# A two-layer decoder step: attention operands split into two halves at the accumulator, keys turned by DMA, scores paced by the page transposes, and another mixing ratio for the last recurrence

## The chip, the cores and the metric

One core of one Trainium2 chip. The metric is the device time of one execution in microseconds (us), the median of several executions. Engines: PE (TensorE matmul; PEld is its weight load), DVE (VectorE), ACT (ScalarE), POOL (GpSimd), SP (SyncE, which issues nearly all DMAs).

## What is computed

One inference step of a two-layer decoder, over a prompt of 2048 tokens and 8 decoding sequences of 4 new tokens each (32 tokens, "the sample"). The parts that matter here, from the reference:

```
qa, fa, ia, ga, qb, kb, vb, gb, fb = _split(h @ w_in, ...)        # layer 0, one input projection
o_a, s_a = gated_linear_chunked(...)                               # HGRN2 recurrence, 4 heads
o_b = fox_attend(qb, kb, vb, log_sigmoid(fb + b_fox))              # 4 heads of 128
out = concatenate([o_a * silu(ga), o_b * silu(gb)]) @ w_out        # layer-0 output projection
...
# fox_prompt: logits = q k^T * scale + c_t - c_s, causal softmax, times v
# fox_sample: the same of 4 new tokens against 16 pages of 128 cached keys per sequence, page_table picks the pages
o, s = gated_linear_chunked(...); return o @ w_out                 # layer 1: GLA, 4 heads of 128 x 256
return rmsnorm(x, final_norm), kb_h, vb_h, ...                     # the keys and values are outputs too
```

All data is f32. Every large product is made of three f16 passes: an operand x is split into hi = f16(x) and lo = f16(x - hi), and `mm3` (L595 to L597) adds hi*hi, hi*lo and lo*hi in f32.

## The kernel before, in words

The program runs through four stages. **Even** (0 to 852 us of the trace): the input projection of layer 0 for the first and then the second half of the tokens, mixed with the HGRN2 recurrences of the four heads (`lin(0)` to `lin(3)`). A projection is a list of units with names: "Bq", "Bk", "Bv" and "Bg" are the attention's query, key, value and gate columns, two units each (a pair of heads). Each unit's PSUM tiles are `pf_Bq...` (features on partitions) or `pt_Bk...`, `pt_Bv...` (tokens on partitions). **Fox** (852 to 1292): the attention. **Layer-0 output projection and layer 1** (1292 to 2150), and **the last output projection with the final norm** (2150 to 2361).

What the even stage does with the attention's operands (`mk_bq`, `mk_bkv`, from L980): a query tile is evicted by ACT as f32 with its scale (L991) and stored feature-major to DRAM (`qTd`). A key or value tile is evicted by DVE (L1020) as f32, stored to its output (L1034) and, for values, to `vd` as well (L1037). Keys are then turned: four PE transposes per pair of token tiles into a PSUM tile `BkT` (L1045), an ACT eviction with scale (L1049), and a store to `kTd` (L1051).

In fox two generators share the engines. `fox_prompt` walks 16 groups (4 heads x 4 blocks G of 512 query tokens). A group's q, k and v are loaded as f32 (`raw_q`, `raw_k`, `raw_v`, L1321) after the first of four score rows of the group ahead, and split on chip at rows 2 and 3: ACT scales v (L1330), ACT makes hi (L1331), POOL makes lo (L1332), each 128x512. An `issue_after` on the last exponential and the last key copy of the sample holds these splits back in the queues. Then come: scores `s` on PE (L1378 on, through `mm3`), bias and row maximum on DVE (L1385), the exponential on ACT (L1393), the scale by one over the sum on POOL (L1401) of a tile `L`, its transposes `pt` on PE (L1421), their split on ACT (`th`, L1428) and DVE (`tl`, L1429), and the product with v into `fo`. `L` tiles live in a pool "P" of 17 buffers. `fox_sample` loads 128 pages of keys and then of values (`pgcache_fox_k`, `pgcache_fox_v`, 256 KB each, L1515), turns the keys by PE (four transposes of one page row make a "turn": `pkt`, L1545), copies them (`kts`, ACT and DVE by turns, L1548 and L1549), multiplies them with the queries (`sc`, L1603) and the probabilities with the values (`pv`, L1684). `until` (L1316) interleaves the two generators by their estimated costs and the ratio FOX_P to FOX_S.

What sets the order: the Python order in which instructions are given to the framework, and a scheduler of the framework that orders each engine's queue by priorities and by its own estimate of readiness; `issue_after(x)` is a hint that an instruction is put behind x in that order, not a wait. Within a queue an engine runs strictly in order, so an instruction that waits holds everything behind it.

Last stage: `mux` (L75) interleaves the last head's recurrence of the second half, `lins[1](3)`, with `third()` (the output projection of the first half, tiles `pt_o`) by LIN3_B to 88000 (L2127). The recurrence's results leave as `py_C133`, `y_C`, are stored to `yT`, come back as `yr`, and are turned into the operand `act` (L1784, L1785) of the last tiles `pt_o`.

## Time and profile before

| | |
|---|---|
| runs of the kernel before | 2357.75, 2358.47, 2360.31 us, median 2358.47 |
| the profiled execution | 2362.66 us, its span in the trace 2361.0 us, mean granted clock 0.988 |
| busy shares over the span | PE 96%, PEld 68%, DVE 59%, ACT 46%, POOL 35%; DMA queue 1 47% |
| instructions | 58204 |

How to read the views. A row of a table of windows gives a stretch's start and end, its length, the busy time (and instruction count) of PE, PEld, DVE, ACT and POOL, the mean granted PE clock as a share of full speed, the mean busy share of the 16 DMA engines (parts in parallel can take it a little over 1), and the GB/s moved. A row of groups gives line, engine, operation, tiles out<-in, shapes and count, then busy us and mean ns of one, then the engine's idle time just before them with what ended it. In a timeline the two first numbers are start and duration in us; idle time before the row stands in brackets. PE matmuls are pipelined: a row's duration contains a latency, so the cost of one in a series is the distance of starts.

### The profile page before, as it was taken

The numbers are of one execution on the slowest core, as the hardware profiler recorded it, in microseconds if no ns is written. First come the engines' busy times: TensorE is split into PE (matmuls) and PEld (weight loads), VectorE is DVE, ScalarE is ACT, GpSimd is POOL, SyncE is SP. The second block draws the span as 40 slices with busy tenths as digits, with TensorE's granted clock in tenths as the row PEclk, the third lists the DMA queues.
The fourth block names the chain that finished last, engine by engine and source line by source line (L and its number), as shares of the span: only waits on it lengthen the run. The fifth ranks groups of instructions, "written<-read, shape, count | busy, mean of one in ns | idle before, by whom it ended". The sixth has DMA issues, their size and how long they took to land. (4 is left out here: it accounts for less than half of the span.)

```text
span 2361.0 us, 58204 instructions
## 1 busy us (share of the span) xinstructions
PE 2267.8 (96%) x23124; PEld 1614.2 (68%) x23124; DVE 1404.2 (59%) x3225; ACT 1090.5 (46%) x2372; POOL 816.5 (35%) x858
## 2 busy tenths in 40 slices
PE   7999999999999999999999999999899999999998
PEld 6677667855655876655446888667677666667877
DVE  7756567536764548566767444366775655557554
ACT  6434354233333127566677443546544544544333
POOL 2333333102212225234557244144552432232222
PEclk9999999999999999999999999999999999999999
DMA  6232235855431276776874778523234431115453
GB/s 199 65 95 74 83 105 157 199 144 157 141 118 60 85 218 214 256 248 204 268 236 141 255 215 244 141 82 117 74 113 109 107 97 57 51 53 167 152 194 148
DMA packets 358003, 344.89 MB, mean 146 GB/s; under 512 B 90993, under 2 KB 300722, under 8 KB 357730
## 3 DMA queue, kind: packets, MB, share of 16 engines
q1 hardware_dynamic: 356226, 336.64, 47.0%
q8 instruction: 182, 2.98, 0.5%
q0 software_dynamic: 1504, 4.52, 0.5%
q14 instruction: 91, 0.75, 0.1%
HBM read 248.73 MB, written 79.63 MB: 139 GB/s over the span
## 5 line engine op out<-in xcount | busy, mean ns | idle before, releaser
L597 PE MATMUL pt_o<-w_o,act 128*128 128x256 f16 x1024 | 281.1, 274 | 4.0 <-DVE act L1785 3.6
L596 PE MATMUL pt_o<-w_o,act 128*128 128x256 f16 x1024 | 281.1, 275 | 1.5 <-POOL w_o L356 1.5
L595 PE MATMUL pt_o<-w_o,act 128*128 128x256 f16 x1024 | 281.2, 275 | 0.9 <-ACT sg1C L652 0.9
L595 PEld LDWEIGHTS <-act 128*128 128x128 f16 x2304 | 227.3, 99 | 39.5 <-DMA act<-xs 5.4
L597 PEld LDWEIGHTS <-act 128*128 128x128 f16 x2304 | 227.4, 99 | 38.0 <-DVE act L1785 5.0
L596 PEld LDWEIGHTS <-act 128*128 128x128 f16 x2304 | 227.4, 99 | 31.5 <-issue 1.5
L595 PE MATMUL pt_Cv<-w_Cv,act 128*128 128x256 f16 (+1 forms) x512 | 142.2, 278 | 3.7 <-DMA act<-xs 3.6
L762 POOL TENSOR_TENSOR kA<-kA,fA 128x512 f32<-128x512 f32 (+1 forms) x56 | 79.0, 1411 | 186.8 <-PE gl_A L728 139.9
L596 PE MATMUL pt_Cv<-w_Cv,act 128*128 128x256 f16 (+1 forms) x512 | 142.1, 278 | 0.0
L597 PE MATMUL pt_Cv<-w_Cv,act 128*128 128x256 f16 (+1 forms) x512 | 142.0, 277 | 0.0
L762 POOL TENSOR_TENSOR kC<-kC,fC 128x512 f32<-128x512 f32 (+1 forms) x56 | 83.7, 1495 | 154.8 <-PE gl_C L728 106.1
L1393 ACT ACTIVATE L<-L,nm,kc 128x512 f32<-128x512 f32 (+3 forms) x160 | 118.2, 741 | 34.7 <-DVE nm L1391 31.4
L1401 POOL TENSOR_SCALAR L<-L,nm 128x512 f32<-128x512 f32 (+3 forms) x160 | 99.1, 634 | 63.5 <-DVE nm L1397 22.9
L1428 ACT ACTIVATE th<-pt 128x512 f16<-128x512 f32 (+3 forms) x159 | 80.5, 528 | 63.0 <-PE pt L1421 62.2
L1429 DVE TENSOR_TENSOR tl<-pt,th 128x512 f16<-128x512 f32 (+3 forms) x159 | 94.5, 608 | 21.9 <-ACT th L1428 20.9
L1421 PE MATMUL pt<-ident,L 128*128 128x128 f32 x544 | 91.3, 279 | 6.8 <-POOL L L1401 4.1
L1421 PEld LDWEIGHTS pt<-ident,L 128*128 128x128 f32 x544 | 66.8, 143 | 32.9 <-DVE tl L1429 8.3
L1545 PEld LDWEIGHTS pkt<-ident,pgcache_fox_k 128*128 128x128 f32 x512 | 58.3, 142 | 41.7 <-issue 25.1
L1879 ACT ACTIVATE vC<-pt_Cv,kc 128x512 f32<-128x512 f32 (+1 forms) x40 | 23.9, 599 | 133.8 <-PE pt_Cv L597 133.8
L1545 PE MATMUL pkt<-ident,pgcache_fox_k 128*128 128x128 f32 x512 | 75.7, 281 | 6.0 <-DVE kts L1549 3.9
L595 PE MATMUL pt_Av<-w_Ai,act 128*128 128x256 f16 x256 | 71.1, 278 | 0.5 <-ACT act L590 0.5
L596 PE MATMUL pt_Av<-w_Ai,act 128*128 128x256 f16 x256 | 70.9, 277 | 0.4 <-DVE w_Ai L349 0.4
(957 smaller groups left out, 6751.4 us busy)
## 6 DMA issues: line engine op xcount, KB each, us to landing
pgcache_fox_k<-in_cache_fox_k SPq DMA_DIRECT2D x128, 256.0 KB, 4.3
pgcache_fox_v<-in_cache_fox_v SPq DMA_DIRECT2D x128, 256.0 KB, 4.0
yr<-yT SPq DMA_DIRECT2D x16, 1024.0 KB, 7.1
x1d<-xo SPq DMA_DIRECT2D x48, 256.0 KB, 3.9
wr_Aqf<-in_w_in_even SPq DMA_DIRECT2D x64, 128.0 KB, 3.2
wr_o<-in_w_out_even SPq DMA_DIRECT2D x32, 256.0 KB, 6.1
xo<-in_x_prompt SPq DMA_DIRECT2D x32, 256.0 KB, 3.6
wr_Cv<-in_w_in_odd SPq DMA_DIRECT2D x32, 256.0 KB, 3.9
```

The source lines that it names most:

```text
L595: nc.tensor.matmul(ps, lh[0], rh[0], start=first, stop=False)
L596: nc.tensor.matmul(ps, lh[0], rh[1], start=False, stop=False)
L597: return nc.tensor.matmul(ps, lh[1], rh[0], start=False, stop=last)
L762: nc.gpsimd.tensor_tensor(kv[:, :, 0], kv[:, :, 0], t1.to_broadcast([P, nb, w]), ALU.mult)
L1393: self.last_exp = nc.scalar.activation(lt[:, :w], lt[:, :w], AF.Exp, bias=nm[:, 0:1], scale=ib, accum_out=nm[:, 2 + j : 3 + j])
L1401: nc.gpsimd.tensor_scalar(lt[:, :w], lt[:, :w], nm[:, 1:2], 2.0**14, ALU.mult, ALU.mult)
L1421: nc.tensor.transpose(pt[:, w : w + P], rows[b][s // 4][0][:, (s % 4) * P : (s % 4 + 1) * P], self.ident)
L1428: nc.scalar.activation(th[:, a:w], pt[:, a:w], AF.Copy),
L1429: nc.vector.tensor_tensor(tl[:, a:w], pt[:, a:w], th[:, a:w], ALU.subtract)))
L1545: nc.tensor.transpose(pk[:, j * P : (j + 1) * P], pgs[j][:, h * P : (h + 1) * P], self.ident)
L1879: r = nc.scalar.activation(v[h][:, g : g + cnt], ps[:, :, :256], AF.Copy, scale=c)
```

## The change

- **Even stage.** A query tile is split where it leaves PSUM: ACT writes hi as f16, DVE writes lo as f16 (one `scalar_tensor_tensor`), one DMA stores both to `qd`. A key or value tile keeps its f32 eviction and output store, and gets two ACT and two DVE instructions per pair of token tiles (each 128x256) that write hi and lo; they go token-major to `kd` and `vd`. The PE transposes and the ACT eviction of the prompt's keys are gone; those of the 32 sample tokens stay. A new column `cu` holds the product of the two scales. The sample's q, k and v are kept in f32 (`qs`, `ks`, `vs`).
- **Fox loads.** q and v are loaded as f16 pairs by plain DMAs, k by `dma_start_transpose` of a 512 x 256 f16 block per group, all without a split on chip. Pool "P" has 20 buffers, q 3, k 6, v 6.
- **Order in fox.** A score tile is put behind the page transposition that lies PKLAG = 16 turns back (`self.pks`). The hints on the splits are gone with them.
- **Last stage.** LIN3_B goes from 21000 to 27000: more steps of the recurrence per step of the output projection.

The core of the diff:

```diff
+PKLAG = 16
-LIN3_B = 21000.0
+LIN3_B = 27000.0
...
-                            nc.scalar.activation(t[:, :m], ps, AF.Copy, scale=self.fsc["q", hp][0])
-                            store_cols(self.qTd[h], t, c0, m)
+                            up, few = self.fsc["q", hp][0], max(0, c0 + m - HALF)
+                            u = t.bitcast(F16).rearrange("p (x t) -> p x t", x=2)[:, :, : m - few]
+                            nc.scalar.activation(u[:, 0], ps[:, : m - few], AF.Copy, scale=up)
+                            nc.vector.scalar_tensor_tensor(u[:, 1], ps[:, : m - few], up, u[:, 0], ALU.mult,
+                                                           ALU.subtract)
...
                     nc.vector.tensor_scalar(t[:m, g % 2 : g % 2 + cnt], ps[:, :, :256], c, None, ALU.mult)
+                    if m == P:
+                        u = held[1]
+                        for j in range(cnt):
+                            src = ps[:, j, :256].rearrange("p (h d) -> p h d", h=2)
+                            hi, lo = (u[:, g % 2 + j, :, x] for x in range(2))
+                            nc.scalar.activation(hi, src, AF.Copy, scale=self.cu[which, hp])
+                            nc.vector.scalar_tensor_tensor(lo, src, self.cu[which, hp], hi, ALU.mult, ALU.subtract)
...
-                    if which == "k":
+                    if which == "k" and m < P:
                         pk = pps.tile([P, 2, 256], F32, tag="gr", name=f"BkT{hf}{hp}{g}")
...
-            fx = Pool(f0, {"vh": 5, "vl": 5, "P": 17, "th": 4, "tl": 4, "sg": 3, "y": 1},
-                      Pool(f1, {"raw": 6, "caus": 1, "qh": 2, "ql": 2, "kh": 5, "kl": 5, "cb": 2, "st1": 12, "cm": 2}))
+            fx = Pool(f0, {"v2": 6, "P": 20, "th": 4, "tl": 4, "sg": 3, "y": 1},
+                      Pool(f1, {"caus": 1, "q2": 3, "k2": 6, "cb": 2, "st1": 12, "cm": 2}))
...
-        if scale is not None:
-            nc.scalar.activation(r, r, AF.Copy, scale=scale)
-        nc.scalar.activation(hi, r, AF.Copy)
-        nc.gpsimd.tensor_tensor(lo, r, hi, ALU.subtract)
...
+            nc.sync.dma_start(q, self.qd[h][:, :, gs])
+            nc.sync.dma_start_transpose(k, self.kd[gs, h].rearrange("t x d -> t (x d)"))
             bias(h, G)
...
-                self.last_pe = self.mm3(ps[:, :w], q, [x[:, :w] for x in K[h, j]], True, True)
+                with ExitStack() as st:
+                    if len(self.pks) > PKLAG:
+                        st.enter_context(self.tc.issue_after(self.pks[-1 - PKLAG].ins))
+                    self.last_pe = self.mm3(ps[:, :w], q, [x[:, :w] for x in K[h, j]], True, True)
...
-                nc.tensor.transpose(pk[:, j * P : (j + 1) * P], pgs[j][:, h * P : (h + 1) * P], self.ident)
+                last = nc.tensor.transpose(pk[:, j * P : (j + 1) * P], pgs[j][:, h * P : (h + 1) * P], self.ident)
+            self.pks.append(last)
```

Three places in the order. The first is SP's queue at the start of fox, where the loads of the first groups stand ahead of the first page (`raw_...` and `k2_...` are loads for head and block, `out_fox_v_p` the outputs of the last value tiles, `cb` a bias row). Before:

```order
L1321 DMA raw_q00_10833<-qTd_71 128x512
L1321 DMA raw_k00_10835<-kTd_72 128x512
L1347 DMA cb0_10837<-cbd_75 128x512
L1321 DMA raw_v00_10839<-vd_74 128x4x128
L1321 DMA raw_q01_10870<-qTd_71 128x512
L1321 DMA raw_k01_10872<-kTd_72 128x512
L1034 DMA out_fox_v_p<-Bv112_10693 128x2x256
L1037 DMA vd_74<-Bv112_10693 128x2x256
```

And of the change:

```order
L1352 DMA q2_00_10916<-qd_71 128x2x512
L1353 DMA_TRANSPOSE k2_00_10917<-kd_72 128x2x512
L1057 DMA out_fox_v_p<-Bv110_10702 128x2x256
L1345 DMA cb0_10921<-cbd_78 128x512
L1352 DMA q2_01_10940<-qd_71 128x2x512
L1353 DMA_TRANSPOSE k2_01_10941<-kd_72 128x2x512
L1059 DMA vd_73<-Bvs110_10703 128x2x512
L1345 DMA cb0_10921<-cbd_78 128x512
L1352 DMA q2_02_11018<-qd_71 128x2x512
L1353 DMA_TRANSPOSE k2_02_11019<-kd_72 128x2x512
L1057 DMA out_fox_v_p<-Bv112_10761 128x2x256
```

Key loads became transposing DMAs; three more of them (`k2_03`, `k2_10`, `k2_11`) follow, so that six stand in SP's queue ahead of the first page load, while the value loads moved behind pages.

The second is PE's queue in the middle of fox, where the page turns `pkt203` and `pkt210` come; `sc` are the sample's products, `fo` and `pt` the prompt's. Before, the page turns follow one another with only the sample's work between:

```order
L1634 MATMUL sc1_12413<-suf_11679,sel_11608 32x128 x7
L1545 MATMUL pkt203_13180<-ident_58,pgcache_fox_k08_13127 128x128
L1545 MATMUL pkt203_13180<-ident_58,pgcache_fox_k09_13129 128x128
L1545 MATMUL pkt203_13180<-ident_58,pgcache_fox_k010_13131 128x128
L1545 MATMUL pkt203_13180<-ident_58,pgcache_fox_k011_13133 128x128
L1545 MATMUL pkt210_13265<-ident_58,pgcache_fox_k18_13257 128x128
L1545 MATMUL pkt210_13265<-ident_58,pgcache_fox_k19_13259 128x128
L1545 MATMUL pkt210_13265<-ident_58,pgcache_fox_k110_13261 128x128
L1545 MATMUL pkt210_13265<-ident_58,pgcache_fox_k111_13263 128x128
L1603 MATMUL sc2_13332<-kts200_13140,qz_11093 32x512
```

With the change the prompt's work stands between the same two turns:

```order
L1534 MATMUL pkt203_13198<-ident_58,pgcache_fox_k011_13151 128x128
L601 LDWEIGHTS v2_03_11270
L601 MATMUL fo03_13036<-th03015_13835,v2_03_11270 128x128
L1418 MATMUL pt1000_13968<-ident_58,L100_13044 128x128
L1418 MATMUL pt1000_13968<-ident_58,L110_13297 128x128
L1418 MATMUL pt1000_13968<-ident_58,L120_13522 128x128
L1418 MATMUL pt1001_13977<-ident_58,L110_13297 128x128
L1418 MATMUL pt1001_13977<-ident_58,L120_13522 128x128
L1534 MATMUL pkt210_13283<-ident_58,pgcache_fox_k18_13275 128x128
```

The prompt's score tiles no longer run ahead of the pages, so that their transposes and products are left for this place. Of the 127 gaps between neighbouring page turns, 54 hold no work of the prompt in the order before (the longest run is 16 turns, from `pkt200` on), and 41 with the change (the longest run 6).

The third is PE's queue in the last stage, where the last head's results `py_C133` leave the recurrence among the tiles of the first half's output projection (`pt_o1000` to `pt_o1036`, 16 tiles of 48 matmuls). Before:

```order
L597 MATMUL pt_o1036_31600<-w_o103_30842,act_18943 128x256
L700 MATMUL py_C1330_31588<-ident_58,on_C133_31567 128x128 x2
L595 LDWEIGHTS act_18943
L595 MATMUL pt_o1036_31600<-w_o103_30842,act_18943 128x256
L596 LDWEIGHTS act_18943
L596 MATMUL pt_o1036_31600<-w_o103_30842,act_18943 128x256
L700 MATMUL py_C1331_31594<-ident_58,on_C133_31567 128x128 x2
```

And with the change:

```order
L601 MATMUL pt_o1030_31299<-w_o103_30765,act_18818 128x256
L704 MATMUL py_C1330_31253<-ident_58,on_C133_31232 128x128 x2
L599 LDWEIGHTS act_18818
L599 MATMUL pt_o1030_31299<-w_o103_30765,act_18818 128x256
L600 LDWEIGHTS act_18818
L600 MATMUL pt_o1030_31299<-w_o103_30765,act_18818 128x256
L601 LDWEIGHTS act_18818
L601 MATMUL pt_o1030_31299<-w_o103_30765,act_18818 128x256
```

The last `py_C1331` moved from behind the 29th matmul of `pt_o1036` to behind the 20th of `pt_o1030`: 28 + 48 + 48 + 29 = 153 matmuls of the projection that stood ahead of it now stand behind it.

More of the change, by code (lines that the diff above doesn't have):

```diff
@@ L1350, in loads @@
             gs = slice(G * 512, (G + 1) * 512)
[L1351 to L1352 removed]
+            q, k, v = (fx.tile([P, 1024], F16, tag=x + "2", name=f"{x}2_{h}{G}") for x in "qkv")
+            q, k = (x.rearrange("p (x t) -> p x t", x=2) for x in (q, k))
+            v = v.rearrange("p (c x d) -> p c x d", c=4, x=2)
+            nc.sync.dma_start(q, self.qd[h][:, :, gs])
+            nc.sync.dma_start_transpose(k, self.kd[gs, h].rearrange("t x d -> t (x d)"))
             bias(h, G)
[L1354 removed]
+            nc.sync.dma_start(v.rearrange("p c x d -> p c (x d)"),
+                              self.vd[gs, h].rearrange("(c s) x d -> s c (x d)", s=P))
+            Q[h, G], K[h, G], V[h, G] = ([x[:, 0], x[:, 1]] for x in (q, k, v.rearrange("p c x d -> p x c d")))
             SG[h, G] = fx.tile([P, 512], F32, tag="sg", name=f"fsg{h}{G}")
             nc.sync.dma_start(SG[h, G], self.sgd[h][:, gs])
[L1358 to L1365 removed]
         def scores(h, G, b):
@@ L1449, in fox_prompt @@
         loads(0, 0)
-        for x in "qkv":
-            split(x, 0, 0)
         pv, ns = iter(()), 0
@@ L1456, in fox_prompt @@
                 rows.append((yield from scores(h, G, b)))
-                if j + 1 < len(groups):
-                    if b == 0:
-                        loads(*groups[j + 1])
-                    elif b == 2:
-                        split("q", *groups[j + 1])
-                        split("k", *groups[j + 1])
-                    elif b == 3:
-                        split("v", *groups[j + 1])
+                if j + 1 < len(groups) and b == 0:
+                    loads(*groups[j + 1])
                 for _ in range(ns // 4):
@@ L1525, in fox_sample @@
         vn = one([TS, 512], "vn")
-        for t, d in ((qs, self.qTd), (kn, self.kTd), (sgs, self.sgd)):
-            nc.sync.dma_start(t, d[:, :, T : T + TS].rearrange("h p t -> p h t"))
-        nc.sync.dma_start(vn, self.vd[T : T + TS])
+        for t, d in ((qs, self.qs), (kn, self.ks), (sgs, self.sgd[:, :, T : T + TS])):
+            nc.sync.dma_start(t, d.rearrange("h p t -> p h t"))
+        nc.sync.dma_start(vn, self.vs)
         with self.tc.issue_after(self.last_l.ins):
@@ L1616, in fox_sample @@
                         new.append(turn(c, b, h, pgs))
-                    if h == 2:
-                        self.last_kt = new[-1][1]
                     yield SC_C
@@ L1721, in fox_scale @@
         nc.vector.reciprocal(up, down)
+        self.cu[which, hp] = self.kcol()
+        nc.vector.tensor_scalar(self.cu[which, hp], c, up, None, ALU.mult)
         if which == "v":
```

67 lines of the change are left out of this document (26 added, 41 removed).

## The prediction

> **What bounds the kernel now.** First the page's list of busy times.
>
> ```profile
> span 2361.0 us, 58204 instructions
> PE 2267.8 (96%) x23124; PEld 1614.2 (68%) x23124; DVE 1404.2 (59%) x3225; ACT 1090.5 (46%) x2372; POOL 816.5 (35%) x858
> ```
>
> PE is busy for 96% of the span; the next engine, DVE, for 59%. So there are two ways to gain: take instructions off PE, or take away some of the few per cent in which it stands still or runs slowly. An average hides where these are, so the second view is the table of windows, cut at the stages.
>
> ```profile
> 0.00:852.00 852.00, 826.55 (x9065) 583.64 (x9066) 506.37 (x1167) 313.04 (x702) 227.57 (x219) 0.99 0.42 119
> 852.00:1292.00 440.00, 411.64 (x2914) 245.18 (x2913) 303.21 (x940) 278.09 (x625) 215.98 (x326) 0.98 0.71 229
> 2150.00:2361.00 211.00, 195.51 (x2162) 169.56 (x2160) 118.51 (x231) 78.74 (x196) 59.94 (x67) 0.97 0.51 169
> ```
>
> PE is idle for 25.5 us of the even stage, 28.4 us of fox and 15.5 us of the last stage. The clock column adds to that: at 0.98 over 440 us fox loses another 8.8 us, so that about 37 us is all that shorter waits could give there. Fox is also where the DMA engines are busiest (0.71). The sum below is made against the profiled execution, 2362.66 us. It is 4.2 us above the median of the runs, 2358.47, and I take those 4.2 us off at the end.
>
> **Even stage: transposes out, evictions in.** These groups (0 to 866 us, shapes apart; fox in the two last) carry the prices.
>
> ```profile
> L1045 PE MATMUL BkT<-ident,Bk 128*128 128x128 f32 x64 | 9.9, 276 | 1.1 <-DVE lf L1015 0.6 <-ACT kts_A L845 0.5
> L1049 ACT ACTIVATE BkS<-BkT,kc 128x512 f32<-128x512 f32 x16 | 11.0, 685 | 56.1 <-PE BkT L1045 53.3 <-issue 2.3 <-ACT scT L736 0.5
> L1020 DVE TENSOR_SCALAR Bv<-pt_Bv,kc 128x256 f32<-128x256 f32 x16 | 7.4, 474 | 0.0
> L991 ACT ACTIVATE Bq<-pf_Bq,kc 128x512 f32<-128x512 f32 x8 | 5.5, 688 | 7.3 <-PE pf_Bq L597 7.3
> L1429 DVE TENSOR_TENSOR tl<-pt,th 128x512 f16<-128x512 f32 x112 | 75.5, 686 | 20.6 <-ACT th L1428 19.9
> L1428 ACT ACTIVATE th<-pt 128x512 f16<-128x512 f32 x112 | 64.0, 590 | 46.6 <-PE pt L1421 46.2
> ```
>
> The 64 prompt transposes leave PE. The 276 ns of one contain a latency; what one costs in a series is the distance of starts, which the page transposes show, the same operation on the same shape:
>
> ```profile
> 1002.37 1.07 PE L1603 MATMUL sc<-kts,qz 128*32 128x512 f32 x8 [0.45 <-DVE kts L1549]
> 1003.37 1.09 PE L1545 MATMUL pkt<-ident,pgcache_fox_k 128*128 128x128 f32 x8
> 1004.81 1.09 PE L1545 MATMUL pkt<-ident,pgcache_fox_k 128*128 128x128 f32 x8 [0.35 <-DVE kts L1549]
> 1006.25 1.06 PE L1603 MATMUL sc<-kts,qz 128*32 128x512 f32 x8 [0.35 <-DVE kts L1549]
> ```
>
> Eight take 1.09 us with one latency of about 0.27 at the end, so 0.82 over seven steps, 0.117 each; 64 of them are 7.5 us, of which I take 7, and the 1.1 us that PE waited ahead of them goes too: **-8**.
>
> Added are 64 hi on ACT and 64 lo on DVE (128x256), and 20 lo on DVE for the queries. No row before shows these; the nearest are L1429's lo (686 ns for 128x512) and L1020's 474 ns for 128x256, so a lo of 128x256 is about 0.45 us and 64 are 29 us, and 20 query tiles at about 0.6 are 12 us: 41 us more on DVE. ACT gets 64 x about 0.38 (half of 590, and a fixed part) = 24 us and loses the 11.0 us of L1049. What hides them is PE's own work in the same place:
>
> ```profile
> 360.00:400.00 40.00, 38.04 (x560) 31.95 (x558) 26.02 (x65) 13.82 (x29) 13.24 (x11) 1.00 0.45 135
> 400.00:475.00 75.00, 75.00 (x732) 66.25 (x731) 42.21 (x84) 25.46 (x56) 15.70 (x13) 1.00 0.79 201
> ...
> 360.00:400.00 40.00, 3.31 (x5) 1.00 0.45 135
> ```
>
> The last row is line L1020 alone. From 400 to 475 PE is never idle and DVE has 33 us left; there the lo's are covered. From 360 to 400, where the recurrence's short steps go back and forth between PE and DVE, DVE is busy for 26 of 40 us and an added lo can stand ahead of a step that PE waits for. Five evictions by L1020 stand there and about as many at the matching place of the second half: some ten pairs of lo at 0.9 us, 9 us at most if each is waited for in full; few will be, since three PSUM buffers of the projection stand between. I take **+2**, with 0 and +6 as ends (a gain is excluded: work is only added). Together **-6**.
>
> **Fox, the start.** The timeline and the window of the first microseconds:
>
> ```profile
> 871.00:879.00 8.00, 5.81 (x20) 2.64 (x21) 3.31 (x14) 5.32 (x13) 6.31 (x9) 0.57 1.02 310
> ...
> 867.50 0.22 PE L595 MATMUL s<-h_k,h_q 128*128 128x128 f16 x1 [0.99 <-DVE Bv L1020]
> 872.54 3.06 SPq L1515 DMA_DIRECT2D pgcache_fox_k<-in_cache_fox_k  x6
> 875.33 0.61 PE L597 MATMUL s<-h_k,l_q 128*128 128x512 f16 x1 [0.43 <-POOL l_q L1332]
> 1487.23 2.10 SPq L565 DMA_TRANSPOSE act<-xs  x1
> ```
>
> POOL is busy for 6.3 of 8 us (it splits, and PE waits for its l_q), and the clock is 0.57: 0.43 x 8 = 3.4 us of PE's speed lost. Without splits on chip I take those **-3**. Against that stand the transposing loads. One costs SP about 2.1 us for 128 x 2048 (`act<-xs`), so about 1.2 for a k block of half that size, against 0.4 for a plain load: six ahead of the first page load are +5 us in a queue that had gaps. Their packets are slower too:
>
> ```profile
> 1475.00:1490.00 15.00, 13.84 (x116) 10.87 (x115) 5.12 (x21) 5.75 (x11) 2.31 (x2) 1.00 1.08 201
> 1001.00:1013.00 12.00, 9.81 (x76) 5.88 (x76) 4.77 (x8) 3.68 (x7) 0.00 (x0) 1.00 0.88 307
> ```
>
> Where transposes and plain loads of layer 1 mix, a full share (1.08) moves 201 GB/s; with pages alone 0.88 moves 307. Per unit of DMA time that is 186 against 349. So a transposed k block of 256 KB takes about twice the 0.75 us of a plain one, 16 blocks some 12 us of DMA time more in a stage that has 0.29 x 440 = 128 us free. Only at the start, with the engines full, is it late: **+2** for pages and first keys (ends 0 and +13, worked out with the slower rival). [...] The start comes to **-1**.
>
> **Fox, the sample alone.** In the rows from 1002 to 1006 above, page turns and scores of the sample have PE for themselves: one step of four turns takes 3.88 us (1002.37 to 1006.25), in which PE starts 8 score and 16 page matmuls, 1.0 + 2 x 0.94 = 2.8 us of its own work. So each step loses 1.1 us, 0.28 a turn, waiting for kts, the copy. In the order 54 of 127 gaps between turns held no prompt work before, and 41 after: 13 x 0.28 = 3.6, **-4** (ends 0 and -10, if the short runs that remain cost less than the long one).
>
> **Fox, ACT and POOL.** What PE waits for, by groups (852 to 1292 us):
>
> ```profile
> L1421 PE MATMUL pt<-ident,L 128*128 128x128 f32 x544 | 91.3, 279 | 6.8 <-POOL L L1401 4.1 <-DVE tl L1429 2.6
> L1545 PE MATMUL pkt<-ident,pgcache_fox_k 128*128 128x128 f32 x512 | 75.7, 281 | 6.0 <-DVE kts L1549 3.9 <-DVE nm L1396 0.8 <-ACT kts L1548 0.7
> L595 PE MATMUL fo<-th,h_v 128*128 128x512 f16 (+3 forms) x174 | 59.0, 339 | 4.6 <-ACT th L1428 3.3 <-DVE mx L1385 0.9 <-DVE fy L1444 0.3
> L596 PE MATMUL s<-l_k,h_q 128*128 128x512 f16 (+3 forms) x160 | 56.0, 351 | 1.2 <-POOL l_k L1332 1.2
> L597 PE MATMUL s<-h_k,l_q 128*128 128x512 f16 (+3 forms) x160 | 55.3, 354 | 0.4 <-POOL l_q L1332 0.4
> ...
> L1330 ACT ACTIVATE raw_v<-raw_v,kc 128x512 f32<-128x512 f32 x16 | 11.4, 712 | 4.4 <-DMA raw_v<-vd 4.4
> L1331 ACT ACTIVATE h_q<-raw_q 128x512 f16<-128x512 f32 x16 | 9.9, 619 | 8.0 <-DMA raw_q<-qTd 8.0
> L1332 POOL TENSOR_TENSOR l_k<-raw_k,h_k 128x512 f16<-128x512 f32 x16 | 18.6, 1160 | 0.0
> ```
>
> The splits are 16 x (0.712 + 3 x 0.62) = 41 us of ACT's 278 and 16 x 3 x 1.16 = 56 us of POOL's 216, each a block of one to three microseconds in an in-order queue that `th` and `L` also pass. PE's waits for those two engines' results are 4.1 + 3.3 + 1.2 + 0.4 = 9.0 us. I take all of them, **-9**: what later delays put in their place is balanced by waits that stand as "DVE tl" but come from ACT's `th` just before. The ends are 0 (PE is late for DVE next, which keeps its 303 us) and -25 (the 37 us of idle time and lost clock, less the 3 at the start and the 8.5 that these rows put down to DVE: 2.6, 0.9, 0.3, 3.9 and 0.8).
>
> **Last stage.** The output projection stops twice, on the operand of the last recurrence's results.
>
> ```profile
> 2271.05 0.27 PE L596 MATMUL pt_o<-w_o,act 128*128 128x256 f16 x1
> ...
> 2272.04 0.27 PE L596 MATMUL pt_o<-w_o,act 128*128 128x256 f16 x1
> 2274.98 0.40 PE L597 MATMUL pt_o<-w_o,act 128*128 128x256 f16 x1 [2.67 <-DVE act L1785]
> ...
> 2277.38 0.39 PE L597 MATMUL pt_o<-w_o,act 128*128 128x256 f16 x1 [0.94 <-DVE act L1785]
> 2270.00:2282.00 12.00, 8.28 (x50) 5.46 (x48) 7.79 (x12) 5.84 (x12) 2.80 (x3) 0.72 0.71 233
> ```
>
> The stops are 2.67 + 0.94 = 3.6 us, and the clock after them, 0.72 over 12 us, costs 3.4 more. A projection matmul takes 0.11 us (nine starts from 2271.05 to 2272.04), so with 153 of them put behind `py_C1331` it comes 16.8 us earlier, more than the stop is long. Both go: **-7** (ends -8, and +1 if the denser recurrence pays as much in small waits among `pt_o1012` to `pt_o1016`, where the order now crowds its steps). [...]
>
> **The sum.** -6 - 1 - 4 - 9 - 7 = -27: 2362.7 - 27 = 2335.7, less 4.2 for the median: **2331.5 us**.
>
> **The rivals.** *Fox gives nothing back* (25%): PE is busy for 94% of it, and the groups name DVE as often as ACT and POOL; the splits may go where nobody waited, and the gaps filled in one place open in another. Then -6 - 1 - 7 = -14 remain: 2344.5. For it speaks that DVE loses nothing in fox; against it the l_k and l_q waits, which have no other cause. *Fox gives all* (8%): the whole -25 and -10, with the rest -14: 2309.5. *The edits don't reach what ends the stages* (8%): the even stage's end is set by the recurrence's steps, so that PE waits where it transposed (0 in place of -6), fox gives nothing, and the denser mixing pays its gain back as waits (0): 2357.5, no change. *Slower, by the transposing loads* (14%): at 860 to 885 us the DMA engines and SP are full. If SP spends the whole 2.1 - 0.4 us more on each of six transposes, the first page comes 10 us later than 872.54 and lands after its turn in PE's order; since the scores are now placed behind page turns, the prompt isn't there to fill, and PE stops for up to 10 us and pays 3.4 more at the low clock: +13. If the pages then run at the pace of the DMA, the 12 us of slower packets come on top, and nothing of -4 and -9 is gained: -6 - 3 + 13 + 12 - 7 = +9, 2367.5. It decides from where late pages and slower packets together cost more than the 16 us (6 + 3 + 7) that are gained all the same. Against it speaks that SP has gaps in that stretch and that a k block is half of `act<-xs`.
>
> **How the numbers follow.** The forecast has 45%. Faster by over 0.2% (4.7 us, about what a measurement of this kernel can tell from no change) are the forecast and the first two rivals: 0.78; same 0.08; slower 0.14. The range leaves out the slower rival alone and what lies beyond the ends: from 2308, just below the forecast with fox at its ends of -25 and -10, to 2358, the no-change rival. The small bounds (+6 for evictions, +1 for the last stage) lie inside it.
>
> **What would show it.** Even: no `BkT` rows but the sample's, the first score of fox near 861 in place of 867.50, and the idle time of 360 to 400 no larger. Fox: `pt` and `fo` rows with less idle before them, POOL under 165 us, fewer stretches at 0.5 clock, the step of 3.88 us seldom seen. Last stage: no wait on `act` L1785 near the end. The forecast is wrong if DVE's idle time in fox shrinks while PE's stays, if `pkt` rows wait on DMA, or if new half-clock dips come in the even stage.

## The result, and the profile after

The changed kernel takes 2351.77 us (median of 18 runs, 2347.61 to 2357.16) against 2358.11 us before (18 runs). The ratio is 0.9973, with a 95% interval of 0.9965 to 0.9982: faster by 6.3 us, where 27 had been forecast. The profiled execution took 2352.48 us. It lies 0.7 us above its median, that of before 4.6 above its own, so the two traces differ by about 4 us more than the medians do.

The page after, its span and busy times:

```profile
span 2350.6 us, 58140 instructions
PE 2252.2 (96%) x23060; PEld 1603.4 (68%) x23060; DVE 1442.3 (61%) x3313; ACT 1075.6 (46%) x2360; POOL 759.4 (32%) x810
```

Shares alone look like the forecast: 64 matmuls less, 57 us off POOL, 38 more on DVE, and 15 off ACT, whose 41 us of splits in fox went while evictions came in the even stage. Where the time went is seen only in a table by stage. Below are windows of before, cut where something starts: first score of fox, first `fo` product (about 880 us), first tile of the output projection, first `pt_Cv` of layer 1, first tile of the last stage.

```profile
867.00:880.00 13.00, 8.91 (x35) 3.77 (x35) 7.77 (x37) 7.51 (x18) 9.16 (x14) 0.74 1.02 320
880.00:1292.00 412.00, 388.23 (x2746) 228.66 (x2747) 291.58 (x899) 268.05 (x603) 203.68 (x309) 0.98 0.69 224
1292.00:1468.00 176.00, 171.99 (x1637) 152.12 (x1634) 81.44 (x103) 77.12 (x127) 76.33 (x53) 1.00 0.78 243
1468.00:2151.00 683.00, 663.09 (x7357) 464.16 (x7358) 395.17 (x786) 343.54 (x722) 236.64 (x194) 0.99 0.33 94
2151.00:2361.00 210.00, 194.51 (x2158) 169.07 (x2156) 118.02 (x230) 78.74 (x196) 59.94 (x67) 0.97 0.51 168
```

The same cuts after:

```profile
860.00:880.00 20.00, 9.88 (x41) 4.81 (x38) 9.41 (x42) 6.30 (x16) 5.35 (x12) 0.67 1.06 304
880.00:1283.00 403.00, 383.98 (x2749) 228.10 (x2747) 291.57 (x894) 237.41 (x543) 151.66 (x261) 0.99 0.72 227
1283.00:1468.00 185.00, 173.06 (x1638) 152.03 (x1636) 82.01 (x105) 79.59 (x131) 80.33 (x56) 0.99 0.74 227
1468.00:2149.00 681.00, 662.89 (x7359) 464.38 (x7358) 394.97 (x786) 343.36 (x723) 236.75 (x194) 0.99 0.33 94
2149.00:2350.00 201.00, 189.83 (x2155) 167.36 (x2153) 117.39 (x230) 78.86 (x196) 59.85 (x67) 0.99 0.53 176
```

The first column of lengths is the story. The even stage ends 7 us earlier (860 for 867). The first stretch of fox takes 20 us for 13, at nearly the same PE work (9.9 and 8.9 busy), and gives that back. The rest of fox takes 403 for 412. The first output projection takes 185 for 176, again at the same work (173 busy), and gives that back too. Layer 1 is as it was, and the last stage takes 202 for 210 (the last window after ends 0.6 us ahead of the trace). Two gains of 7 and 9 us were thus each returned at the next stage's start; the last stage has no next one. Each length is read from one execution: in the traces below that have the same fox code as the change, the rest of fox takes 402.9 to 406.6 us, and with the mixing ratio alone on the kernel before 416.6 in place of 412.6, so a single length is good to some 4 us.

The first give-back, in DVE's, PE's and SP's timelines after:

```profile
860.48 0.75 DVE L1036 TENSOR_SCALAR Bv<-pt_Bv,kc 128x512 f32<-128x512 f32 x1 [2.35 <-PE pt_Bv L601]
862.88 0.48 DVE L1043 SCALAR_TENSOR_TENSOR Bvs<-pt_Bv,kc,Bvs 128x256 f16<-128x256 f32 x1 [0.47 <-ACT Bvs L1042]
863.62 0.48 PE L599 MATMUL s<-k,q 128*128 128x384 f16 x1 [2.69 <-DVE mx L1382]
868.06 0.96 SPq L1504 DMA_DIRECT2D pgcache_fox_k<-in_cache_fox_k  x2
869.12 0.38 SPq L1059 DMA_DIRECT2D vd<-Bvs  x1
873.24 0.56 DVE L1382 CUSTOM_DVE_ANT_0 L<-s,cb 128x384 f32<-128x384 f32 x1 [7.27 <-DMA vd<-Bvs]
874.37 0.29 PE L599 MATMUL s<-k,q 128*128 128x128 f16 x1 [6.83 <-DVE mx L1382]
```

The last value tile is evicted from 860.48 on and its split is complete at 863.36. PE's first stop of 2.69 us lies there: DVE evicts and splits before it comes to the first row maximum. The store of the split is issued only at 869.12. A logit tile `L` lies in memory that the store still reads, so DVE waits for it until 873.24, and PE waits for DVE, 6.83 us. Before, the same wait of DVE was 1.09 us long:

```profile
871.97 0.56 DVE L1385 CUSTOM_DVE_ANT_0 L<-s,cb 128x384 f32<-128x384 f32 x1 [1.09 <-DMA vd<-Bv]
```

### The profile page after: what moved, and what is told of

Read it like the earlier page. It is cut to its first block, busy times and chain, and to the rows that moved or that the text cites. A ratio compares the mean times of both kernels' runs of the same rounds, so it can differ in the third digit from the quotient of the medians.

```text
span 2350.6 us, 58140 instructions
## 1 busy us (share of the span) xinstructions
PE 2252.2 (96%) x23060; PEld 1603.4 (68%) x23060; DVE 1442.3 (61%) x3313; ACT 1075.6 (46%) x2360; POOL 759.4 (32%) x810
## 4 chain that ended last, share of the span: by engine, by line
PE 73%; DVE 9%; DMA 6%; ACT 4%; issue 4%; POOL 3%; SPq 2%; DVEq 0%; POOLq 0%; ACTq 0%
PE pt_o L599 2%; PE pt_o L600 2%; PE pt_o L601 2%; PE pkt L1534 2%; PE pt L1418 2%; PE pt_Cv L599 2%; PE pt_Cv L600 2%; PE pt_Cv L601 2%; PE sc L1593 1%; PE pv L1672 1%; DVE scT L747 1%; PE pf_Ag L601 1%; PE pf_Ag L600 1%; PE pf_Ag L599 1%; PE pf_Bq L601 1%
## 5 line engine op out<-in xcount | busy, mean ns | idle before, releaser
L1365 POOL TENSOR_TENSOR cm<-cb,caus 128x128 f32<-128x128 f32 x64 | 29.1, 455 | 170.0 <-DVE mx L1382 119.8
L599 PE MATMUL pt_Bk<-w_Bk,act 128*128 128x256 f16 x256 | 70.7, 276 | 1.9 <-DVE Bvs L1043 1.6
```

The costliest lines, as they stand in the source:

```text
L599: nc.tensor.matmul(ps, lh[0], rh[0], start=first, stop=False)
L1365: self.last_cm = nc.gpsimd.tensor_tensor(cm, cb[:, tb * P : (tb + 1) * P], caus, ALU.add)
```

## The experiments

Times of the runs below are ratios to the kernel before, measured beside it. "First score to first fo" is read from PE's timeline of each run: 12.1 us before, 19.3 after.

**The mixing ratio put back.**

```diff
-LIN3_B = 27000.0
+LIN3_B = 21000.0
```

> The changed kernel with LIN3_B back at 21000. In its trace the lead over the kernel before grew from 2.4 us at the first tile of the last stage to 10.0 us at the end. If that 7.6 us is the denser mixing, this run is slower than the changed kernel by 7 to 8 us (about 2359 us), its output projection stops again on act near the end, and the stages ahead of 2150 us stay as they are. Rival: the stop moves with anything that shifts the stage and the mixing is worth nothing; then the run stays at about 2352 us.

Measured: 2360.15 us, ratio 1.0005 (0.9994 to 1.0017), so the mixing is worth 0.32%, 7.5 us, and everything else in the change together about nothing. (By the medians measured side by side, 2360.15 and 2355.56, the rest even lost 4.6 us; the size is good to a few us.) PE's waits between 2200 and 2300 us show the stop again, which the changed kernel doesn't have:

```profile
PE pt_o L601 <- DVE act L1775: 4.5, 2, 3.6
```

**The mixing ratio alone**, on the kernel before (LIN3_B 27000, nothing else).

> The kernel before with LIN3_B at 27000 and nothing else. With LIN3_B back at 21000 the rest of the change took as long as the kernel before (ratio 1.0005), so if the parts add up this run has the whole gain: ratio 0.9965 to 0.9975, stop on act near the end gone, all stages ahead of 2150 us as before within 2 us. Rival: the denser mixing needs the other parts; then under 3 us.

Measured: 0.9981 (0.9969 to 0.9992), 4.5 us. The stop is gone, the last stage is 204.6 us long and the stages ahead are as before, though fox was 4 us longer in this trace. The expected size isn't reached; the intervals of the two estimates, 4.5 and 7.5 us, overlap.

**The last value stores from another queue.**

```diff
-                        nc.sync.dma_start(dst.rearrange("(g s) h x d -> s g (h x d)", s=P),
+                        eng = nc.scalar if which == "v" and hf == 1 and hp == 1 else nc.sync
+                        eng.dma_start(dst.rearrange("(g s) h x d -> s g (h x d)", s=P),
```

> The changed kernel with the split stores of the last value unit issued from ACT's queue in place of SP's. Theory 1: the six transposing key loads fill SP's queue, the last of these stores is issued some 4 us after its data is there, and DVE's wait for it (7.3 us, on memory that the new score tiles take over) stops PE for 6.8 us and halves its clock. Then DVE's wait falls below 3 us, the first fo product comes near 872 in place of 879.6 us, and fox ends 6 to 10 us earlier. Theory 2 (rival): the DMA engines are full of slow transposing packets and the store lands late wherever it is issued; then the wait stays above 5 us. Theory 3, on what comes after: the hand-over to layer 1 is a chain of stores and loads that gives back any lead; then the first pt_Cv stays near 1467 us and the time near 2351; without it the time is 2342 to 2346.

Measured: 0.9974 (0.9959 to 0.9988), as the changed kernel, and 19.0 us from first score to first fo. The wait moved to another engine: the store, now in ACT's queue, was issued at 872.19 all the same, and ACT's next exponential stood behind it.

```profile
872.19 0.37 ACTq L1060 DMA_DIRECT2D vd<-Bvs  x1
872.60 0.49 ACT L1391 ACTIVATE L<-L,nm,kc 128x128 f32<-128x128 f32 x1 [6.82 <-DMA cb<-cbd]
```

The trace puts ACT's 6.82 us down to a load of `cb`, which the store has no use for. Its records of semaphores tell why. In the trace of the changed kernel SP's 1335 DMAs go through eight completion semaphores by turns, and in all 830 cases whose landing the trace has, an issue came after the landing of the transfer that had its semaphore before. In this run the DMAs of both queues take turns at them. The store's had been given to a `cb` load that SP issued at 866.75; this landed at 872.11, and the store went out 0.08 us later. In the changed kernel the transfer before it had landed at 868.75, the issue ahead of the store ended at 869.02, and the store went out at 869.12. So the other queue didn't help: in it the store went out only after a load that SP had issued ahead of it had landed. Neither theory was confirmed as it was put.

**Keys loaded without the turn**, a plain DMA of the same bytes (the prompt's attention is computed on unturned keys).

```diff
-            nc.sync.dma_start_transpose(k, self.kd[gs, h].rearrange("t x d -> t (x d)"))
+            nc.sync.dma_start(k.rearrange("p x (c d) -> p (x c) d", d=256), self.kd[gs, h].rearrange("(c s) x d -> s c (x d)", s=P))
```

> The changed kernel with its 16 key blocks loaded by a plain DMA of the same bytes, so the keys are not turned and the prompt's attention is computed on unturned keys. Theory 1: SP gets about 6 us back ahead of the first page and the 7.3 us wait of DVE shrinks to 1 to 3 us. Theory 2: the same, and the DMA share at 843 to 885 us falls too, by more than the store's move alone can explain. Fox shorter by 8 to 12 us if the transposing loads are its whole loss, by under 3 us if they are not. Time 2342 to 2352 us, depending on whether the hand-over gives it back.

Measured: 0.9964 (0.9950 to 0.9979). DVE's wait for `vd<-Bvs` is 1.78 us, and first score to first fo 16.8 us, 2.5 less. The rest of fox is as with the turn (403.7 us). PE's long stop is another one here: it stands still for 6.41 us while ACT, ahead of the last tile's split, waits 7.46 us for an earlier store (`vd<-Bvs`). Turning or not, the start hangs on stores of the last value tiles. So transposing costs little after the start: the whole of it is 0.1%, 2 us, within the intervals.

**No coupling.** PKLAG = 1000 in place of 16.

> The changed kernel without the coupling (PKLAG beyond the number of turns). If the coupling fills the sample's lonely steps as forecast, the stretch of the page turns (884 to 1083 us) gets longer by 3 to 5 us and the rest of fox shorter by less; time 2353 to 2356 us. Rival: the prompt's work only changes its place, and fox takes as long as with it, within 1.5 us.

Measured: 1.0031 (1.0017 to 1.0045), 14 us slower than with it by the ratios and 12 by the medians, where 1 to 4 were expected. First the page turns before, then with the change, then without coupling (groups of the tile `pkt`: ns, and first and last start):

```profile
L1545 PE MATMUL pkt<-ident,pgcache_fox_k x512: 272/273/475, 884.5 to 1082.8; 128*128 128x128 f32 x171
```

```profile
L1534 PE MATMUL pkt<-ident,pgcache_fox_k x512: 272/273/330, 883.8 to 1081.1; 128*128 128x128 f32 x171
```

```profile
L1534 PE MATMUL pkt<-ident,pgcache_fox_k x512: 272/273/332, 884.2 to 1133.4; 128*128 128x128 f32 x171
```

With the coupling the turns end where they did before; without it 52 us later, and the sample's value products start at 1150.6 in place of 1096.7. There the loss lies: PE waits 18.3 us of the rest of fox for value pages, with the coupling 0.3 us.

```profile
PE pv L1672 <- DMA pgcache_fox_v<-in_cache_fox_v: 18.3, 12, 3.4
```

The coupling doesn't fill lonely steps. In PE's order of the traces, 54 of the 127 gaps between turns hold no work of the prompt before, 41 with the change and 29 without the coupling: it makes more of them. PE's waits for the copies `kts` go the same way, 6.5 us before, 4.9 with the change and 2.1 without the coupling. It holds the prompt back, so that the sample's pages keep the pace that they had in the kernel before.

**The coupling on the kernel before**, with LIN3_B at 27000, without the split at PSUM.

```diff
+                with ExitStack() as st:
+                    if len(self.pks) > PKLAG:
+                        st.enter_context(self.tc.issue_after(self.pks[-1 - PKLAG].ins))
```

> The kernel before with the coupling of 16 turns and LIN3_B at 27000, without the split at PSUM, the transposing loads and the larger pool. If the coupling is a gain of its own (without it the changed kernel is 11.7 us slower), this is faster than the kernel before with LIN3_B alone by 4 us or more (ratio under 0.996). Rival: the splits on chip already coupled the prompt to the sample by their own hints, and the coupling adds nothing: within 2 us of it.

Measured: 0.9987 (0.9976 to 0.9999), against 0.9981 without the coupling. The rival holds as to the time: on the kernel before, the coupling adds nothing.

**PE freed just ahead of fox.** The last value unit in two passes (its activations' lo part is left out).

```diff
+                    if nm == "Bv11":
+                        self.nc.tensor.matmul(ps[:n, j], lh[0], rh[0], start=k == 0, stop=False)
+                        self.nc.tensor.matmul(ps[:n, j], lh[0], rh[1], start=False, stop=k == KT - 1)
```

> The changed kernel with the last value unit ahead of fox in two matmul passes in place of three (the lo part of the activations is left out there), 64 matmuls or 7 us of PE less, directly ahead of fox; its DMAs are the same. Theory 2 (the start of fox waits for DMA transfers, which run at full share from 850 us on): the first score comes 7 us earlier, the first fo product stays within 2 us of 879.6, and PE's stops between them grow by 5 to 7 us. Rival (the start is PE's and DVE's own chain): the first fo product comes 5 to 7 us earlier too.

Measured: 0.9926 (0.9906 to 0.9945). The forecast of theory 2 fails as it was put: the first fo product comes 9 us earlier.

```profile
851.97 0.22 PE L599 MATMUL s<-k,q 128*128 128x128 f16 x1 [0.45 <-PE pt_Bv L630]
870.39 0.39 PE L599 MATMUL fo<-th,v 128*128 128x512 f16 x1 [0.16 <-DMA v<-vd]
```

From 851.97 to 870.39 are 18.4 us, near the 19.3 of the change. The start isn't pinned to a fixed time; it moves with the last value tile. But the like length hides another chain. ACT's split of the last tile now waits for an earlier store first, PE stops for 5.08 us behind it, and DVE's later wait for the last store is 3.08 us in place of 7.27:

```profile
855.43 0.47 ACT L1046 ACTIVATE Bvs<-pt_Bv,kc 128x256 f16<-128x256 f32 x1 [4.08 <-DMA vd<-Bvs]
857.70 0.48 PE L599 MATMUL s<-k,q 128*128 128x384 f16 x1 [5.08 <-DVE mx L1386]
```

The issues of the DMAs moved to earlier times along with PE, so this run doesn't show that landing times (the engines' share is 1.03 here) play no part.

**PE freed at the end of fox.** The value products of the last head in two passes (v's lo part is left out; the trace has 54 matmuls less).

> The changed kernel with the value products of fox's last head in two passes (its v lo part is left out): some 43 matmuls or about 8 us of PE less in the last 110 us of fox. If the hand-over is a chain of stores and loads that PE only waits for, fox ends 5 to 8 us earlier but the first pt_Cv of layer 1 stays within 2 us of 1467.6. Rival: PE carries the lead through, and the first pt_Cv and the end come 5 us earlier or more.

Measured: 0.9947 (0.9926 to 0.9967), 6 us below the changed kernel. Fox ended 7.5 us earlier than in the changed kernel's trace (2.9 of them were there at the first fo product), and the first `pt_Cv` 11.8 us earlier. So the hand-over to layer 1 isn't a fixed barrier either, against theory 3.

**Three transposing loads away from the start.**

```diff
+                        if j >= 2:
+                            st.enter_context(self.tc.issue_after(sgd[j - 2].ins))
                         loads(*groups[j + 1])
```

> The changed kernel with the loads of the fourth and later groups put behind the gate load of three groups earlier, so that three transposing loads stand in SP's queue ahead of the first page in place of six. From the first score to the first fo product the kernel before takes 12.1 us and six kernels with the change 16.8 (plain loads) to 20.5 us. Theory 1 (SP's queue, with eight transfers in flight at most, issues the last value store late): this distance falls to 13 to 16 us and the time by 3 to 5 us against the changed kernel (2347 to 2349 us). Theory 4 (the added evictions of the last value tile and the memory that the new score tiles take over from its stores set the start): it stays at 18 us or more and the time at 2352 us.

Measured: 2347.11 us, 0.9956 (0.9938 to 0.9973). First score to first fo is 14.7 us. SP issues the store 0.7 us after its data (865.75), in place of 5.8, and DVE's wait is short:

```profile
866.44 0.38 SPq L1059 DMA_DIRECT2D vd<-Bvs  x1
870.03 0.56 DVE L1382 CUSTOM_DVE_ANT_0 L<-s,cb 128x384 f32<-128x384 f32 x1 [1.76 <-DMA vd<-Bvs]
```

Theory 1 holds for 4.6 of the 7.2 us: the eight traces of this document with six turned loads ahead take 18.4 to 20.5 us, the four with three 13.0 to 14.7. The 0.9 to 2.6 us that remain aren't resolved. The stop of 2.69 us, in which DVE evicts and splits the last tile, is in all four, where the kernel before stopped for 0.99 (ahead of the first score) and 0.47; and the granted clock in the stretch is 0.66 to 0.87 in the four and 0.72 before.

**Seventeen logit tiles.**

```diff
-            fx = Pool(f0, {"v2": 6, "P": 20, "th": 4, "tl": 4, "sg": 3, "y": 1},
+            fx = Pool(f0, {"v2": 6, "P": 17, "th": 4, "tl": 4, "sg": 3, "y": 1},
```

> The changed kernel with 17 buffers for logit tiles in place of 20. If the larger pool is part of the 9 us by which fox is shorter from its first fo product to its end (412.5 before, 403.4 with the change), that grows by 2 us or more; if it is worth nothing, within 1.5 us. The three buffers less also move what lies in the memory that the even stage's tiles leave, so the wait of 7.3 us at the start may change with the layout: under theory 4 it can fall, under theory 1 it stays above 5 us.

Measured: 0.9997 (0.9983 to 1.0010). In the trace the whole gain of fox is gone (412.7 us); windows as above, from the first fo to the end of fox, and the output projection:

```profile
882.00:1295.00 413.00, 387.12 (x2753) 228.39 (x2753) 292.28 (x900) 239.40 (x548) 157.62 (x267) 0.99 0.69 219
1295.00:1473.00 178.00, 171.47 (x1631) 151.65 (x1628) 77.35 (x103) 76.84 (x127) 77.09 (x53) 1.00 0.78 241
```

ACT and POOL are as free as with 20 tiles (239 and 158 us in place of 268 and 204), and fox takes as long as before. The hand-over is 6 us shorter than with 20, so that of the 9 us some 6 are left in the time. DVE's first wait was 8.29 us, so the layout alone didn't help the start.

**Six c2 buffers.** EC2 = 6 in place of 4.

> The changed kernel with six in place of four buffers for the even stage's evicted tiles (tag c2), of which a value pair now takes two. Theory 4: the last tiles have their buffers free and their stores out earlier, and the distance from first score to first fo product falls from 19.3 to under 16 us; the time by 3 us. Theory 1: SP's queue is as long as ever, and it stays at 18 to 20 us.

Measured: 0.9969 (0.9956 to 0.9982); first score to first fo 19.7 us, DVE's wait 7.79. More buffers for the evicted tiles don't help, against theory 4.

**The last y stores from SP**, on top of the late loads.

```diff
+            eng = nc.sync if (h, G) == (NH - 1, 3) else nc.gpsimd
+            eng.dma_start(self.yT[0][NH + h][:, G * 512 + c1 : G * 512 + c2], y[:, c1:c2])
```

> As e9_loads_late, with the two stores of fox's last y tile issued from SP in place of POOL, where they stood behind a scaling that waits 3 to 5 us for a load. From the first output-projection tile to layer 1's first pt_Cv the kernels without the split operands take 173 to 176 us, those with it 178 to 188, e9_loads_late 181.8. If POOL's queue is the cause, this falls to 176 to 178 us and the time by 3 to 5 us against e9_loads_late (2342 to 2344 us). Rival: the chain of loads behind it (yr, then act) is late anyway, or the loss lies in the later chain xo, x1d, x1r, xs; then it stays at 180 to 183 us.

Measured: 2346.28 us, 0.9945 (0.9931 to 0.9960), not told apart from the late loads alone. From the output projection to layer 1: 181.5 us, the rival's value. POOL's queue isn't the cause.

**More logit tiles**, on top of the late loads: 23 with two q buffers, then 22 with three.

> As e9_loads_late, with 23 logit tiles (5 buffers for k and v, 2 for q). Three buffers from 17 to 20 shortened fox from its first fo product to its end by 9 us (412.6 to 403.4). If the number of logit tiles still limits how far scores run ahead, three more give 2 to 6 us again; if 20 was enough, within 1.5 us, and fewer k and q buffers may cost some.

> As e9_loads_late, with 22 logit tiles, 5 buffers for k and v and again 3 for q. In e13_late_p23, two q buffers made one score wait 19.1 us for its q load, which hid what more logit tiles give. If they still limit, fox from its first fo product to its end falls below 400 us (e9_loads_late: 401.6) and the time to 2342 to 2345 us; if 20 was enough, it stays within 1.5 us of 401.6; if the fifth k or v buffer is missed as the third q buffer was, a wait for a load shows on PE and it gets longer.

Measured: 1.0001 (0.9989 to 1.0012) and 0.9955 (0.9939 to 0.9970). The first is spoiled by its q buffers:

```profile
PE s L599 <- DMA q<-qd: 19.1, 1, 19.1
```

The second takes 403.4 us from the first fo to the end of fox, with one wait of 5.4 us for a k load in it. Twenty were enough, or what more tiles give went to that wait.

**The pool on the kernel before**: LIN3_B 27000, 20 logit tiles, and 3 raw buffers in place of 6 to make room.

> The kernel before with LIN3_B at 27000, 20 logit tiles and, to make room for them, 3 buffers for raw loads in place of 6; splits on chip as before. If the pool alone made fox 9 us shorter, its first fo to end falls from 416.6 (with LIN3_B alone) to about 408 and the time is 2343 to 2347 us: then splitting at PSUM only made the room. Rival: the pool helps only with ACT and POOL freed of the splits, or 3 raw buffers hold the loads back; then no gain or a loss.

Measured: 1.0088 (1.0069 to 1.0108), slower. One score waited for a q split, since three raw buffers let the loads run ahead too little:

```profile
PE s L595 <- ACT h_q L1331: 9.0, 1, 9.0
```

That wait doesn't make up the 15 us that fox lost against the mixing ratio alone; waits for `th` grew too (7.9 for 5.0 us), and the clock fell from 0.98 to 0.96. So the run doesn't tell whether the pool alone would do. It shows that before the change there was no room for it without a price.

## Why the prediction was wrong, point by point

Against the profiled execution -27 was forecast and -10.4 came. Of the 16.6 us between, 8.2 are at fox's start (-1 forecast, +7.2 measured), 8.5 in the hand-over from fox to layer 1, to which the prediction gave no term, and 3.9 in the rest of fox (-13 by two terms, -9.1 measured); the even stage, layer 1 and the last stage gave 3.9 more than forecast. The steps that failed are these three.

**Even stage, -6: right.** The first score came at 860.28 in place of 867.50. The added evictions took about what was estimated: `L1043`'s lo 478 ns where 0.45 us had been taken, ACT's hi 473 where 0.38. They showed elsewhere than expected. From 360 to 400 us PE's idle time grew by half a microsecond only (at a clock of 0.96 in place of 1.00), but from 400 to 475, where PE had never been idle, it now is for 2.3 us, and over 320 to 480 us it grew by 3.1:

```profile
360.00:400.00 40.00, 37.55 (x547) 30.70 (x545) 32.31 (x80) 16.45 (x38) 13.87 (x12) 0.96 0.52 154
400.00:475.00 75.00, 72.72 (x705) 63.53 (x704) 46.32 (x100) 30.11 (x69) 14.41 (x13) 1.00 0.77 187
```

**Fox's start, -1: wrong, it was +7.2.** The splits went, as forecast, but the granted clock was 0.67 from 860 to 880 us, where it had been 0.74 from 867 to 880, and 0.50 from 874 to 880, after a stop of 6.83 us. The step that failed is "+5 us in a queue that had gaps", priced at +2. Those microseconds were counted for the page loads, which weren't late (`pkt` starts at 883.8, before at 884.5). Behind the six transposing loads in SP's queue stood something shorter of time: the last value tile's store. It came 5.8 us after its data, DVE waited 7.27 us for the memory that the store reads, and PE 6.83 us for DVE. Taking three loads away gave 4.6 us back. The rest may go with the added lo's: they were costed at nothing where PE has other work, but behind the last tile there is none. The first point is shown by an experiment; the second is read from the trace and isn't shown. The slower rival had the right place and the wrong victim. Its DMA-bound part didn't come: the page turns end at 1081.1 (1082.8 before), and the rest of fox is as long with plain loads as with turned ones.

The term also took a turned block's transfer at twice a plain one's, an estimate from two windows, one of them a mixture. That didn't show: the turned blocks landed in 4.0 us (median of the 8 of 16 whose landing the trace has; 4.7 for the f32 key loads before, 10 of 16), and with plain loads the kernel gained 0.1%, within its interval. What took longer is the issue: SP's queue is taken for 1.3 us by each, against 0.38 by the store above (ns: least, median, most):

```profile
L1353 SPq DMA_TRANSPOSE k<-kd x16: 1226/1312/2248, 844.3 to 1189.9; - x16
...
DMA to landing us min/median/max: 3.2/4.0/5.2
```

**The sample's lonely steps, -4: wrong mechanism.** PE's waits for `kts` fell by 1.6 us, and it wasn't the coupling that took lonely steps away (29 of them without it, 41 with it). What it does is hold the prompt back: the turns end at 1081.1 with it and at 1133.4 without, where PE then waits 18.3 us for value pages. It is worth 12 to 14 us to the changed kernel and nothing to the kernel before, where the hints on the splits, which the change removes, stand in the code. That these did its work is the reading that fits both runs; the hints alone were not taken away. Of their removal no term spoke.

**ACT and POOL freed, -9: the size came by luck, the cause was wrong.** From the first fo on, fox got 9.1 us shorter (412.6 to 403.5), and the -4 would have to be in that too. With 17 logit tiles it takes 412.7, ACT and POOL being as free as with 20: freeing them gave nothing by itself. Nor did the waits go that the term was made of, or not all: from the first fo on, those for POOL's `l_k` and ACT's `h_q` went (1.0 us), that for POOL's `L` fell from 2.3 to 0.9, but PE still waits as long for ACT's `th` (3.3 us before, 3.8 after). The waits for DVE's `tl`, which the prediction had put down to late `th` in part, fell from 5.6 to 1.7.

```profile
PE fo L599 <- ACT th L1425: 3.8, 2, 3.0
```

With 17 tiles `L` costs 3.8 and `tl` 3.0. So the gain needs the larger pool, which the prediction named in no term; splitting at PSUM made room for it by freeing the f32 tiles' memory. Whether the pool would do without the freed engines wasn't shown.

**The hand-over, in no term: +8.5 in the trace.** With the split operands the stretch from the output projection to the first `pt_Cv` takes 180 to 188 us in all runs but two: 177.5 with less PE work ahead of fox, 178.5 with 17 logit tiles. Without the split it takes 173 to 176, and 179.9 in the run with three raw buffers. In the changed kernel PE is idle there for 11.9 us in place of 4.2, at the same matmuls. In the first 31 us it waits for operands of the projection (`act` and `w_o`), 5.6 us in place of 1.7, and at the end for a turned load of layer 1, 6.36 us in place of 2.46. Before, then after:

```profile
1468.17 0.29 PE L595 MATMUL pt_Cv<-w_Cv,act 128*128 128x272 f16 x1 [2.46 <-DMA act<-xs]
1467.57 0.41 PE L599 MATMUL pt_Cv<-w_Cv,act 128*128 128x272 f16 x1 [6.36 <-DMA act<-xs]
```

It isn't POOL's queue and not a fixed barrier. The step that failed is that a lead at the end of fox was taken to reach layer 1 whole. These two waits took 7.7 of the 8.5 us; which loads or stores ahead of them set them stays open.

**Last stage, -7: right.** From 210 to 202 us; 7.5 us by the ratios, 4.5 on the kernel before. No wait on `act` is left. The clock there is 0.99 in place of 0.97.

The sum was thus, in us of the traces, -7.2 +7.2 -9.1 +8.5 -1.8 (layer 1) -7.9: -10.4 between the profiled executions (2361.0 to 2350.6 in span), 6.3 by the medians. The forecast took the three gains and none of the returns. The best version run is the change with three key loads moved behind the first pages, 0.9956, or 0.9945 with the last y stores from SP as well (10 to 13 us below the kernel before); its trace shows the start's loss shrunk to 2.6 us.

## What to carry to other kernels

Here gains of 7 and 9 us were given back, 7.2 and 8.5 us, at the next stage's start: follow the last tile of a stage through its eviction, its store and the memory it hands over, and ask what stands ahead of that store in the issuing queue. Price loads by what is queued behind them, too: with six turned loads ahead no page was late (turns from 883.8 us, before from 884.5), but the store behind them was issued 5.8 us after its data, and with three 0.7. When a change frees memory and spends it on buffers, give the buffers a term of their own, and when it removes instructions, look whether their ordering hints went with them.

## What the runs showed of the hardware that was not expected

A store moved from SP's to ACT's queue wasn't issued earlier (9.0 us after the first score, against 8.8), and the engine's own next instruction came after 6.82 us of idle time: here, issuing from a compute engine put the wait for another transfer's landing into that engine's order. And 7 us of matmuls taken away directly ahead of fox brought 11 us in the ratios (0.9973 to 0.9926); the two intervals allow 6 to 16, so that it is more than the matmuls take isn't shown.
